# Four weight buffers of a matmul stream, moved to other addresses modulo 512 bytes

## The chip, the cores and the metric

The kernel runs on one core of one Trainium2 chip. The metric is the device time of one execution in microseconds, as the median of several runs. Beside the runs stands one execution that the hardware profiler recorded: its span is the time from its first to its last instruction, and every duration below comes from it.

## The reference

The kernel computes one layer of a trunk for a generative model: a gated linear recurrence over 2048 latent tokens and 256 context tokens of width 1024 (8 heads of 128, both directions), and behind it a gated feed-forward layer with a convolution over three positions. Cut to what matters here, the first part projects all tokens with five weight matrices a head and scans the result in chunks:

```python
def prep(h):
    q, zf_fwd, zf_bwd, v, g = jnp.split(h @ w_in, 5, axis=-1)
    q = heads(jax.nn.silu(q)); v = heads(v)
    for d, zf in enumerate((zf_fwd, zf_bwd)):
        f = lb[d] + (1.0 - lb[d]) * jax.nn.sigmoid(zf)
        logf.append(heads(jnp.log(f))); k.append(heads(1.0 - f))
    return q, k, v, logf, g

lat = lat + g1 * (rmsnorm(o, g_gain) * silu(g)) @ w_out
lat = lat + g2 * (silu(gate) * val) @ w_down      # gate, val: conv of h @ w_up
return rmsnorm(lat, final_g)
```

All of it is float32.

## The kernel before

**Matmuls in three products.** A float32 matrix is split into a high part and the rest (`split`, L77 to L81: ScalarE rounds it to float32r, VectorE subtracts), and a product is made of three float32r matmuls that add into one PSUM tile: high by high, high by rest, rest by high. In the scan these are L470, L471 and L472 of `step`: the weights `w[:, 0, k]`, `w[:, 0, k]` and `w[:, 1, k]` are the stationary operand (128 x 128), the tokens' high part, rest and high part stream past them (512 columns for a unit of four latent token tiles, 256 for the context).

**The stages.** About the first 1230 us of the span are the scan (`mixer_scan`): for two halves of the latent tokens and eight heads, five projections to a head (`project`: eight steps of k, so 24 matmuls of 512 columns), and between their steps small products: transposes (`turned`, `values`), scores inside a chunk (L673), states (L703) and outputs (L725, L728). What comes when is written out: `tick` runs an agenda after each step of three matmuls. Then comes the mixer's output (`mixer_out`, matmuls L1246 to L1248, again with transposes and small products between), to about 1489 us; then the up-projection of the feed-forward layer (`acc_mm`, L1113 to L1116, with the convolution on the other engines), to about 2305 us; then the down-projection (`product`, L1743 to L1745).

**Where the operands lie.** Tiles come from pools that stack up in SBUF. The scan's weights have the pool `wp` with four buffers of 8192 bytes a partition, `[128, 2, KT, 128]`: high and rest, eight k, 128 columns, so that every stationary operand is a run of 512 bytes and starts at the same residue modulo 512 as its buffer. The tokens lie in four blocks of 16384 bytes, `TOK = [128, UT, 2, 4, 128]` (four token tiles, high and rest, four k, 128 columns), in the pool `hp`; a moving operand is four runs of 512 bytes, 4096 bytes apart. By the addresses of the built program both the buffers of `w` and the blocks of `tok` (and the context's `cxt`) start at 96 modulo 512. In the mixer's output the stationary operand `ghl` starts at 352 and the moving `wo` at 96 (for the first of 16 token tiles the stationary tiles are `gh` and `gl`, at 96); in the up-projection the weights start at 96 and the moving operands at 352; in the down-projection the stationary `mh`, `ml` at 352 and the moving `w` at 96.

**What stands around the change.** The pool `lp` lies just below `wp` and holds one tile, `stg`. It outlives the scan, and the pools of the mixer's output begin where it ends. Above `wp` lie the scan's other pools (`hq`, `fix`, `gp`, `xp`). Buffers of `wp` are made in `load_w` (L186) and `split_head0` (L244); late in the scan two of them serve once more as `wraw` (L824), raw weights of the output projection on their way to being split.

Of the kernel before, what the change touches and what calls it, by code (L numbers as in the profile page):

```python
# [11 lines left out]
F32 = mybir.dt.float32  # L12
F32R = mybir.dt.float32r
# [8 lines left out]
D = 1024  # L22
# [3 lines left out]
KT = 8  # L26
# [10 lines left out]
V_CW, V_CB = 0, 132  # L37
V_CN = 176


UT = 4
NS = 4 * UT
# [3 lines left out]
def body(ctx, tc, a, out):  # L46
# [31 lines left out]
    def split(h, l, src):  # L78
        i = act.activation(h, src, AF.Copy)  # L79
        j = dve.tensor_tensor(l, src, h.bitcast(F32), OP.subtract)  # L80
        return i.ins, j.ins  # L81
# [13 lines left out]
    def pool_(stack, name, bufs=1, **kw):  # L95
        return stack.enter_context(tc.tile_pool(name=name, bufs=bufs, reuse_waits="tile", **kw))
# [56 lines left out]


    lp = pool_(ch, "lp")
    c1 = ctx.enter_context(ExitStack())
    wp = pool_(c1, "wp", 4)
    hq = pool_(c1, "hq")
# [23 lines left out]
    def x_tile(xt, t):  # L182
        src, r = (a["x"], t) if t >= 0 else (a["ctx"], t + 2)
        sp.dma_start(xt, src[r * 128:(r + 1) * 128])

    def load_w(h, ty):  # L186
        raw = rawp.tile([128, D], F32, name="raw", tag="raw")
        sp.dma_start(raw, a["w_in"][h, ty])
        w = wp.tile([128, 2, KT, 128], F32R, name="w", tag="w")
        split(w[:, 0], w[:, 1], raw.rearrange("p (k n) -> p k n", k=KT))  # L190
        return w

# [29 lines left out]
    with ExitStack() as c0:  # L222
# [19 lines left out]
        head0 = {}  # L242

        def split_head0(ty, raw):  # L244
            head0[ty] = w = wp.tile([128, 2, KT, 128], F32R, name="w", tag="w")
            return split(w[:, 0], w[:, 1], raw.rearrange("p (k n) -> p k n", k=KT))

        pool.memset(silp, 0.0)
# [21 lines left out]
        for k in range(KT):  # L270
            for c in range(4):
                n = 2 * k + c // 2
# [3 lines left out]
        with tc.issue_after(squared[-1]):  # L276
            made = split_head0(2, head_raw[2])
# [21 lines left out]
        def split_ctx(g):  # L299
            b = cxt[:, g // 2, :, :, 2 * (g % 2):2 * (g % 2) + 2]  # L300
            return split(b[:, :, 0], b[:, :, 1], hmc[g].rearrange("p k s n -> p s k n"))

        made = evict_ctx(0)
        order = [(evict_ctx, 1), (split_ctx, 0), (evict_ctx, 2), (split_ctx, 1), (split_head0, 1),
                 (evict_ctx, 3), (split_ctx, 2), (split_ctx, 3)]
        for f, g in order:
# [6 lines left out]
        with behind_of(made):  # L313
            for t in range(4):
                norm_begin(staged[t], late_junk, gp)
                if t == 1:
                    split_head0(3, head_raw[3])
            norm_end()
# [88 lines left out]
    def mixer_scan():  # L407
# [499 lines left out]
        def head(g, h):  # L907
            w = head0 if g == h == 0 else {}

            def weight(ty):  # L910
                if ty not in w:
                    w[ty] = load_w(h, ty)
                return w[ty]
# [190 lines left out]
    def cols(u, odd):  # L1104

        return u[:, 1:1 + HALF].rearrange("p (j o n) -> p j o n", o=2, n=128)[:, :, odd]
# [332 lines left out]
    wp = pool_(ctx, "wp")  # L1439
# [152 lines left out]
    for g, (half, s, n, q, pairs) in enumerate(todo):  # L1592
# [8 lines left out]
        w, r = pairs[q].w.pop(LEFT[n]), rhs[n]  # L1601
# [9 lines left out]
        elif n == "T1":  # L1611
# [3 lines left out]
            i = dve.tensor_tensor(cols(uvs[q], 1), u2s[q], z, OP.add).ins  # L1615
# [315 lines left out]
```

## Time and profile before

| What | Value |
|---|---|
| median of 3 runs | 2730.86 us (2729.72 to 2731.76) |
| profiled execution, span | 2729.5 us |
| TensorE clock granted in it | 0.997 |
| HBM read, written | 293.23 MB, 114.57 MB |
| DMA packets | 229104, 410.56 MB, mean 150 GB/s |

The stages in the profiled execution, by a view that cuts the span into stretches (busy us of each engine, in brackets how many instructions; then clock, share of the DMA engines, GB/s):

```profile
50.00:610.00 560.00, 558.35 (x4360) 481.58 (x4359) 351.35 (x548) 222.28 (x390) 88.17 (x236) 1.00 0.27 85
610.00:1229.00 619.00, 618.90 (x4730) 517.29 (x4729) 414.50 (x580) 193.03 (x334) 101.76 (x222) 1.00 0.41 130
1229.00:1489.00 260.00, 257.50 (x1376) 218.54 (x1375) 225.90 (x462) 156.83 (x358) 42.32 (x36) 1.00 0.87 310
1489.00:2305.00 816.00, 815.84 (x3599) 674.98 (x3598) 645.54 (x732) 378.49 (x519) 314.10 (x338) 1.00 0.33 108
2305.00:2729.50 424.50, 416.47 (x1833) 343.32 (x1831) 322.78 (x443) 166.34 (x254) 9.23 (x16) 1.00 0.70 232
```

The first number behind each stretch is its length, then come TensorE's matmuls, its weight loads, VectorE, ScalarE and GpSimd. How the profile is to be read: PE is TensorE's matmul row, PEld its weight loads, DVE VectorE, ACT ScalarE, POOL GpSimd, SP the engine that issues most DMAs. A row of the groups reads: line, engine, operation, output from inputs, shape, count, then busy us and mean ns of one, then idle time before and what ended it. The end of a matmul is modelled, so its recorded duration is longer than the time until the next one starts; the starts are as recorded.

### The profile page before, as it was taken

To read this page: it belongs to the slowest core of one execution; us is meant where nothing else is said; L and a number is where in the kernel's file an instruction comes from. 1 tells how busy PE (TensorE), PEld (TensorE's weight loads), DVE (VectorE), ACT (ScalarE), POOL (GpSimd) and SP (SyncE) were. 2 spreads that over 40 slices of the span, in tenths; PEclk is the share of its full clock that TensorE was granted. 3 is DMA by queue.
4 is the path that set the end of the run, shared out by engine and by line. 5 is a ranking of instruction groups with operands and counts; after the bars stand their busy time and mean duration, and the time that the engine had idled before them with its cause. 6 is when DMAs were issued, how large, how long until landed. Compare 5 with 4: busy or idle time off the path is not lost.

```text
span 2729.5 us, 41987 instructions
## 1 busy us (share of the span) xinstructions
PE 2698.7 (99%) x16060; PEld 2252.7 (83%) x16060; DVE 1977.8 (72%) x2803; ACT 1136.9 (42%) x1887; POOL 572.9 (21%) x885
## 2 busy tenths in 40 slices
PE   7999999999999999999999999999999999999999
PEld 4888888888888888888888888888888888888887
DVE  4756655556767776668997888777877777578896
ACT  5334444323233233335666444444444444333444
POOL 3211111011111111211211543333434440000001
PEclk8999999999999999999999999999999999999999
DMA  6213323224544443228888232228322234988653
GB/s 240 86 53 105 106 83 97 86 87 163 167 124 137 149 137 113 87 80 297 300 300 344 93 93 82 73 79 307 93 76 79 78 93 137 309 279 289 200 185 131
DMA packets 229104, 410.56 MB, mean 150 GB/s; under 512 B 29604, under 2 KB 137508, under 8 KB 225064
## 3 DMA queue, kind: packets, MB, share of 16 engines
q1 hardware_dynamic: 224152, 398.65, 44.1%
q10 hardware_dynamic: 4752, 9.24, 0.9%
q8 instruction: 126, 2.06, 0.3%
q14 instruction: 74, 0.61, 0.1%
HBM read 293.23 MB, written 114.57 MB: 149 GB/s over the span
## 4 chain that ended last, share of the span: by engine, by line
PE 91%; DMA 3%; DVE 3%; ACT 1%; issue 1%; POOL 1%; SPq 0%; ACTq 0%; POOLq 0%; DVEq 0%
PE z L470 11%; PE z L472 11%; PE z L471 11%; PE y L1744 4%; PE y L1743 4%; PE y L1745 4%; PE zc L1113 3%; PE zc L1116 3%; PE zc L1115 3%; PE zd L1113 3%; PE zd L1115 3%; PE zd L1116 3%; PE za L1116 3%; PE za L1115 3%; PE za L1113 3%; PE kv L703 2%
## 5 line engine op out<-in xcount | busy, mean ns | idle before, releaser
L470 PE MATMUL z<-tok,w 128*128 128x512 f32 x1280 | 516.4, 404 | 0.0
L472 PE MATMUL z<-tok,w 128*128 128x512 f32 x1280 | 501.0, 391 | 0.0
L471 PE MATMUL z<-tok,w 128*128 128x512 f32 x1280 | 500.6, 391 | 0.0
L80 DVE TENSOR_TENSOR w<-raw,w 128x512 fp32r<-128x512 f32 (+1 forms) x258 | 237.2, 922 | 131.7 <-ACT w L79 127.8
L472 PEld LDWEIGHTS z<-tok,w 128*128 128x128 f32 x1280 | 240.4, 188 | 52.1
L470 PEld LDWEIGHTS z<-tok,w 128*128 128x128 f32 x1280 | 240.8, 188 | 45.7 <-issue 1.7
L471 PEld LDWEIGHTS z<-tok,w 128*128 128x128 f32 x1280 | 241.1, 188 | 43.9 <-DVE tok L80 0.2
L79 ACT ACTIVATE w<-raw 128x512 fp32r<-128x512 f32 (+1 forms) x258 | 194.8, 760 | 132.9 <-PE zd L1116 75.9
L1743 PE MATMUL y<-w,mh 128*128 128x512 f32 x600 | 233.4, 390 | 1.2 <-ACT X L1777 1.2
L1744 PE MATMUL y<-w,mh 128*128 128x512 f32 x600 | 233.6, 389 | 0.2 <-DVE w L80 0.2
L1745 PE MATMUL y<-w,ml 128*128 128x512 f32 x600 | 233.4, 389 | 0.0
L546 DVE TENSOR_TENSOR_SCAN S<-F,d 128x528 f32<-128x528 f32 (+1 forms) x80 | 91.3, 1144 | 119.1 <-ACT F L525 118.9
L80 DVE TENSOR_TENSOR w<-s,w 128x512 fp32r<-128x512 f32 x126 | 121.5, 967 | 57.2 <-ACT w L79 56.3
L75 POOL TENSOR_TENSOR rs<-rs,mhalf 128x1 f32<-128x1 f32 (+3 forms) x53 | 61.9, 1168 | 417.7 <-DVE rs L74 417.7
L79 ACT ACTIVATE w<-s 128x512 fp32r<-128x512 f32 x126 | 78.5, 628 | 150.5 <-POOL s L1181 83.5
L1113 PE MATMUL zc<-rT,w 128*128 128x512 f32 x352 | 137.1, 390 | 0.2 <-DMA rT<-rhs1T 0.2
L1116 PE MATMUL zc<-rT,w 128*128 128x512 f32 x352 | 136.9, 389 | 0.0
L1115 PE MATMUL zc<-rT,w 128*128 128x512 f32 x352 | 136.9, 389 | 0.0
L1743 PEld LDWEIGHTS y<-w,mh 128*128 128x128 f32 x600 | 112.6, 188 | 25.8 <-ACT X L1777 2.1
L1744 PEld LDWEIGHTS y<-w,mh 128*128 128x128 f32 x600 | 112.6, 188 | 23.9 <-DVE w L80 0.6
L1745 PEld LDWEIGHTS y<-w,ml 128*128 128x128 f32 x600 | 112.6, 188 | 23.3
L1116 PE MATMUL za<-rB,w 128*128 128x512 f32 x336 | 130.7, 389 | 0.0
(359 smaller groups left out, 6259.0 us busy)
## 6 DMA issues: line engine op xcount, KB each, us to landing
raw<-in_w_up_dram SPq DMA_DIRECT2D x88, 512.0 KB, 4.0
raw<-in_w_in_dram SPq DMA_DIRECT2D x80, 512.0 KB, 4.0
lr<-m SPq DMA_DIRECT2D x49, 512.0 KB, 5.2
m<-r SPq DMA_DIRECT2D x66, 256.0 KB, 4.3
spare<-in_w_ada_dram SPq DMA_DIRECT2D x32, 512.0 KB, 4.2
kq<-stash SPq DMA_DIRECT2D x15, 1024.0 KB, 8.0
og<-stash SPq DMA_DIRECT2D x30, 512.0 KB, 5.3
u<-in_w_down_dram SPq DMA_DIRECT2D x51, 256.0 KB, 3.5
```

What stands on the lines that cost most here:

```text
L79: i = act.activation(h, src, AF.Copy)
L80: j = dve.tensor_tensor(l, src, h.bitcast(F32), OP.subtract)
L470: pe.matmul(z, w[:, 0, k], h, start=k == 0, stop=False, skip_group_check=True)
L471: pe.matmul(z, w[:, 0, k], l, start=False, stop=False, skip_group_check=True)
L472: stepped_pe[:] = [pe.matmul(z, w[:, 1, k], h, start=False, stop=k == KT - 1, skip_group_check=True).ins]
L546: dve.tensor_tensor_scan(flat(S[:, d]), flat(F[:, d]), flat(d1[:, 0:ns]), 0.0, OP.mult, OP.max)
L1113: pe.matmul(o, w[:, 0, k], r[:, :, 0, k], start=start and k == 0, stop=False, skip_group_check=True)
L1115: pe.matmul(o, w[:, 0, k], r[:, :, 1, k], start=False, stop=False, skip_group_check=True)
L1116: i = pe.matmul(o, w[:, 1, k], r[:, :, 0, k], start=False, stop=k == 3, skip_group_check=True)
L1743: pe.matmul(z, lh, rh, start=start, stop=False, skip_group_check=True)
L1744: pe.matmul(z, lh, rl, start=False, stop=False, skip_group_check=True)
L1745: pe.matmul(z, ll, rh, start=False, stop=stop, skip_group_check=True)
```

## The change

Three things. The pool `lp` gets one more tile, `gap`, of 64 float32 (256 bytes) a partition, ahead of `stg`; nothing reads or writes it. The buffers of `w` become 16 float32 (64 bytes) longer, and `w_tile` hands out the first 2048 elements of one in the old shape. With that the four buffers begin 256 bytes higher, and each 64 bytes further modulo 512 than the one before: at 352, 416, 480 and 32, while `tok` and `cxt` stay at 96. All scan tiles above the weights begin 512 bytes higher; the tiles of the mixer's output above `lp` begin 256 bytes higher.

```diff
+W_SHIFT, W_STEP = 64, 16
+
 UT = 4
...
     lp = pool_(ch, "lp")
+    lp.tile([128, W_SHIFT], F32, name="gap", tag="gap", bufs=1)
     c1 = ctx.enter_context(ExitStack())
     wp = pool_(c1, "wp", 4)
...
+    def w_tile():
+
+        w = wp.tile([128, 2 * D + W_STEP], F32R, name="w", tag="w")
+        return w[:, 0:2 * D].rearrange("p (i k n) -> p i k n", i=2, k=KT)
+
     def load_w(h, ty):
         raw = rawp.tile([128, D], F32, name="raw", tag="raw")
         sp.dma_start(raw, a["w_in"][h, ty])
-        w = wp.tile([128, 2, KT, 128], F32R, name="w", tag="w")
+        w = w_tile()
         split(w[:, 0], w[:, 1], raw.rearrange("p (k n) -> p k n", k=KT))
         return w
...
         def split_head0(ty, raw):
-            head0[ty] = w = wp.tile([128, 2, KT, 128], F32R, name="w", tag="w")
+            head0[ty] = w = w_tile()
             return split(w[:, 0], w[:, 1], raw.rearrange("p (k n) -> p k n", k=KT))
```

The built program has the same instructions in the same order on every engine; lines below the edit move by two to eight, and the waits are the same but for one DMA, the load of `conv` (L1374), which lies over other tiles of the scan than before.

## The prediction

> **What bounds the kernel now.** I read the page's engine shares first, then the chain of waits, then the groups of TensorE instructions kept apart by shape, and last the timeline of single matmuls. The first three lines of the page and of the clock view say which engine counts:
>
> ```profile
> PE 2698.7 (99%) x16060; PEld 2252.7 (83%) x16060; DVE 1977.8 (72%) x2803; ACT 1136.9 (42%) x1887; POOL 572.9 (21%) x885
> PE 91%; DMA 3%; DVE 3%; ACT 1%; issue 1%; POOL 1%; SPq 0%; ACTq 0%; POOLq 0%; DVEq 0%
> core 0: 2729.5 us, clock 0.997
> ```
>
> TensorE is busy 99% of the span, it makes 91% of the chain that ended last, and its clock is granted in full. So an edit that removes no matmul and no wait can only act through the pace of the matmuls, and a nanosecond on each of the scan's 3840 is worth 3.8 us. The groups, with mean ns of one behind the comma:
>
> ```profile
> L470 PE MATMUL z<-tok,w 128*128 128x512 f32 x1280 | 516.4, 404 | 0.0
> L472 PE MATMUL z<-tok,w 128*128 128x512 f32 x1280 | 501.0, 391 | 0.0
> L471 PE MATMUL z<-tok,w 128*128 128x512 f32 x1280 | 500.6, 391 | 0.0
> L1743 PE MATMUL y<-w,mh 128*128 128x512 f32 x600 | 233.4, 390 | 1.2 <-ACT X L1777 1.2
> L1113 PE MATMUL zc<-rT,w 128*128 128x512 f32 x352 | 137.1, 390 | 0.2 <-DMA rT<-rhs1T 0.2
> L1246 PE MATMUL y<-wo,ghl 128*128 128x512 f32 x240 | 96.0, 400 | 1.9 <-ACT ghl L79 1.6 <-DVE lat L1255 0.3
> L1248 PE MATMUL y<-wo,ghl 128*128 128x512 f32 x240 | 94.1, 392 | 0.0
> L1247 PE MATMUL y<-wo,ghl 128*128 128x512 f32 x240 | 93.6, 390 | 0.0
> L1246 PE MATMUL y<-wo,gh 128*128 128x512 f32 x16 | 6.4, 402 | 0.0
> ```
>
> All of these stream 512 columns past 128x128 weights. I call offset the weights' start less the moving operand's start, modulo 512, both from the addresses that the built program assigns. Before the change it is 0 in the scan (both begin at 96), and 256 in the up-projection L1113 (weights 96, moving 352), in the down-projection L1743 (352 and 96) and in the mixer's output L1246 to L1248 with ghl (352 and 96). The tempting reading is that the scan's 404/391/391 against 390 elsewhere is a collision at offset 0. But the mixer's output stands at offset 256 and shows 400/390/392, the scan's pattern, and its 16 matmuls with gh at offset 0 show 402 where ghl has 400. What the scan and the mixer's output share is not the offset but the 128-column transposes and products put between their matmuls, which the other two stages lack. The medians say that nothing is slow throughout (min/median/max ns):
>
> ```profile
> L470 PE MATMUL z<-tok,w x1280: 387/389/504, 49.4 to 1229.2; 128*128 128x512 f32 x183
> L1246 PE MATMUL y<-wo,ghl x240: 387/389/498, 1246.2 to 1461.3; 128*128 128x512 f32 x120
> ```
>
> A matmul's end is modelled, its start is not, so I take the pace from starts. The first and the last of 37 matmuls in an undisturbed stretch of the scan, of 37 in the up-projection, and of 5 with 256 columns:
>
> ```profile
> 1195.10 0.39 PE L471 MATMUL z<-tok,w 128*128 128x512 f32 x1
> 1203.26 0.39 PE L471 MATMUL z<-tok,w 128*128 128x512 f32 x1
> ```
>
> ```profile
> 1700.23 0.39 PE L1113 MATMUL zb<-rT,w 128*128 128x512 f32 x1
> 1708.39 0.39 PE L1113 MATMUL zc<-rT,w 128*128 128x512 f32 x1
> ```
>
> ```profile
> 601.06 0.28 PE L471 MATMUL z<-cxt,w 128*128 128x256 f32 x1
> 601.54 0.28 PE L472 MATMUL z<-cxt,w 128*128 128x256 f32 x1
> ```
>
> Scan at offset 0: 8.16 us over 36 steps, 226.7 ns. Up-projection at offset 256: the same 8.16 us over 36 steps. The settled pace does not differ by 0.3 ns. With 256 columns a step is 0.48 / 4 = 120 ns, so 256 columns more cost 106.7 ns and a fixed part of 226.7 - 2 x 106.7 = 13.3 ns sits in every matmul at both offsets.
>
> The unsettled steps come after small products. Two such stretches, of the scan (offset 0) and of the mixer's output (offset 256), each from its third large matmul on:
>
> ```profile
> 1184.75 0.40 PE L472 MATMUL z<-tok,w 128*128 128x512 f32 x1
> 1184.98 0.40 PE L470 MATMUL z<-tok,w 128*128 128x512 f32 x1
> 1185.22 0.39 PE L471 MATMUL z<-tok,w 128*128 128x512 f32 x1
> ...
> 1186.83 0.39 PE L472 MATMUL z<-tok,w 128*128 128x512 f32 x1
> ```
>
> ```profile
> 1325.16 0.40 PE L1248 MATMUL y<-wo,ghl 128*128 128x512 f32 x1
> 1325.40 0.40 PE L1246 MATMUL y<-wo,ghl 128*128 128x512 f32 x1
> 1325.63 0.39 PE L1247 MATMUL y<-wo,ghl 128*128 128x512 f32 x1
> ...
> 1327.24 0.39 PE L1248 MATMUL y<-wo,ghl 128*128 128x512 f32 x1
> ```
>
> Nine steps take 2.08 us in both, 231.1 ns each, and then both fall into 226.7. So the settling costs 4.4 ns a step for some ten steps, and it runs alike at offsets 0 and 256, with a moving operand in four pieces (tok) and in one (wo).
>
> **The change part by part.** It adds no instruction and removes none. Engine by engine the built programs list the same instructions in the same order; only line and buffer numbers differ.
>
> - The four weight buffers now begin at 352, 416, 480 and 32 modulo 512 against the tokens' 96: offsets 256, 320, 384 and 448. By the program 1008 of the 3840 scan matmuls read the first buffer and 2832 the other three. For the first buffer the trace has the answer: offset 256 is what the up-projection, the down-projection and the mixer's output have, so its matmuls stay at 226.7 ns settled and 231.1 while settling. Gain 0.
> - Offsets 320, 384 and 448 do not occur before with 512-column matmuls, so their cost is bounded from both sides. Gain at most: the whole fixed part, 13.3 ns x 2832 = 37.7 us. Loss at most: the larger steps of the settling kept up for good; both stretches hold a step of 0.24 us, and at that every time it is 13.3 ns x 2832 = 37.7 us the other way. I take 0, by the row that is nearest: going from offset 0 to 256 moved neither the settled pace nor the settling, and the 128-column products stand at other offsets without a mark of it:
>
> ```profile
> L703 PE MATMUL kv<-v,kt 128*128 128x128 f32 x512 | 67.9, 275 | 0.5 <-ACT sk L709 0.4
> L728 PE MATMUL o<-v,at 128*128 128x128 f32 x256 | 49.5, 275 | 0.0
> L362 PE MATMUL oi<-Sb,kq 128*128 128x128 f32 x240 | 29.3, 275 | 0.0
> ```
>
> Their offsets are 384 (kt 128, v 256), 448 (at 192, v 256) and 256 (kq 352, Sb 96), and all three take 275 ns. They are float32 with 128 columns, where the scan's are float32r with 512, so they make the price likely, not certain.
> - The split on ScalarE and VectorE writes w as often and in the same runs of 4 KB, on engines that are 42% and 72% busy and hold 1% and 3% of the chain. Price 0.
> - Behind the weights all scan tiles move by 512 bytes, so modulo 512 they stand as before. The stage after the scan starts its pool 256 bytes later; of its operands only xn (transposed) and gl of the first token tile change their residue, 128 and 16 matmuls. At 4.4 ns each that is at most 0.6 us.
> - One wait differs: the conv load L1374 now overlaps other scan tiles and waits for VectorE and TensorE where it waited for transfers.
>
> ```profile
> SPq L1374 <- DMA stash<-so: 9.9, 1, 9.9
> PE y L1246 <- ACT ghl L79: 1.6, 1, 1.6
> ```
>
> On SP's queue it stands ahead of the stash loads of the mixer's output, which themselves wait for the last stash stores; nothing reads conv until the FFN. If the queue comes free sooner, the most to win is TensorE's one idle moment there, 1.6 us; if later, the same is lost again. I take 0.
>
> Sum: 2729.5 us span + 0. The runs' median is 2730.86, 1.4 us above this execution's span, and that is what lies around it: 2729.5 + 1.4 = **2730.9 us**. A change of under 0.2% (5.5 us) is what a measurement of this kernel can't tell from none.
>
> **The rivals.**
>
> *The collision is real and goes.* Then the scan's excess over 389 ns vanishes. For L471 and L472 it is 2 ns x 2560 = 5.1 us; with L470's 15 ns x 1280 = 19.2 us it is 24.3 us. Time 2706 to 2726. For it: the scan is the one stage at offset 0 with a high mean. Against it: the mixer's output at offset 256 has the same excess, and L470's part is mostly the first matmul behind small products, whose record starts early while it waits its turn. Chance 0.15.
>
> *The fixed part is the collision.* If weight reads and moving reads meet at offsets 0 and 256 alike and miss each other at the three new ones, 13.3 ns x 2832 = 37.7 us go, and with the 456 context matmuls on those buffers 6.1 us more: 2687 to 2693. For it: 13.3 ns are there in every large matmul and no row tells their cause, and every offset in those rows is a multiple of 256. Against it: nothing in the trace varies with the offset. Chance 0.12. The Trainium skill ("TensorE: Matmul & The Clock Gate", section "Back-to-back issue gap") gives N / 2.4 + 2.5 ns for a warm isolated gap, 215.8 at 512 columns; the trace has 226.7, 10.9 more, and by that page as an estimate 2832 x 10.9 = 30.9 us would be free to win (2700). Against this rival and the next stands the skill's "SBUF — State Buffer", section "A bandwidth-pool intuition that's wrong (but worth ruling out)": weights have a second read port independent of the moving operand's. By that rule the time stays at 2730.9; the equal 226.7 ns at two offsets agree with it.
>
> *The new offsets keep the stream unsettled (slower).* The settled pace is a state that the stream falls into after some ten steps. If at 320, 384 or 448 it does not fall into step, the 2832 matmuls run at the settling's mean: 4.4 ns x 2832 = 12.5 us, 2743; at its 0.24 us steps 37.7 us, 2769. It decides from 1.9 ns a matmul (5.5 us). For it: the pace visibly depends on how the stream starts. Against it: it settled at both offsets seen. Chance 0.20.
>
> That the change doesn't do what it says I exclude: the built program has the four addresses.
>
> **How the numbers follow.** No change 0.53, first rival 0.15, second 0.12, third 0.20. Faster is 0.15 + 0.12 = 0.27, the same 0.53, slower 0.20. The likeliest case by itself spans 2726 to 2736. The range goes down to 2706, the foot of the first rival, which leaves out the second (0.12), and up to 2748, which takes in the third from its mean pace and leaves out its worse part (0.08): 0.20 left out.
>
> **What would show it.** In the groups of the changed kernel the three scan lines should read 404/391/391 again, the median 389, and undisturbed stretches 226.7 ns a step on every buffer; after small products nine steps of some 2.08 us. The first rival would show L470 to L472 nearer 389 with L1246 to L1248 unmoved; the second a median under 389 and an up-projection that keeps its own; the third a median over 389. I would be wrong if steps differ between the first buffer and the other three: then the residue by 64 bytes matters, and offsets that are multiples of 256 could not show it.

## The result, and the profile after

The changed kernel is slower by a quarter of a per cent: 2736.57 us (median of 7 runs, 2735.51 to 2739.82) against 2729.72 (7 runs, 2726.86 to 2732.01), a ratio of 1.0026 with a 95% interval of 1.0017 to 1.0036. The profiled execution took 2737.12 us, 2735.1 of them in the span.

The page's engine shares, chain of waits and clock view of the changed kernel (its lines stand eight further down: L470 to L472 are now L478 to L480):

```profile
PE 2704.9 (99%) x16060; PEld 2250.2 (82%) x16060; DVE 1976.2 (72%) x2803; ACT 1137.5 (42%) x1887; POOL 574.5 (21%) x885
PE 92%; DMA 4%; DVE 3%; ACT 1%; issue 1%; POOL 0%; SPq 0%; ACTq 0%; POOLq 0%; DVEq 0%
core 0: 2735.1 us, clock 0.999
```

TensorE is as busy as before, at the full clock, and its share of the chain went from 91% to 92%. Its busy time grew by 6.2 us with the same 16060 matmuls, so the matmuls themselves are slower. The groups by shape say which:

```profile
L478 PE MATMUL z<-tok,w 128*128 128x512 f32 x1280 | 518.9, 406 | 0.0
L480 PE MATMUL z<-tok,w 128*128 128x512 f32 x1280 | 503.9, 394 | 0.0
L479 PE MATMUL z<-tok,w 128*128 128x512 f32 x1280 | 503.9, 394 | 0.0
L1751 PE MATMUL y<-w,mh 128*128 128x512 f32 x600 | 233.4, 390 | 0.7 <-ACT X L1785 0.6
L1121 PE MATMUL zc<-rT,w 128*128 128x512 f32 x352 | 137.0, 389 | 0.2 <-DMA rT<-rhs1T 0.2
L1254 PE MATMUL y<-wo,ghl 128*128 128x512 f32 x240 | 96.0, 400 | 1.4 <-ACT ghl L81 1.4
L478 PE MATMUL z<-cxt,w 128*128 128x256 f32 x192 | 55.9, 291 | 1.3 <-ACT cxt L81 1.3
```

The scan's lines went from 404/391/391 to 406/394/394. The down-projection, the up-projection and the mixer's output, whose operands did not move against each other (but for the `gl` of one token tile), read what they read before within 1 ns. The context's matmuls (256 columns, the last row) became *shorter*; their row before was

```profile
L470 PE MATMUL z<-cxt,w 128*128 128x256 f32 x192 | 57.4, 299 | 1.3 <-ACT cxt L79 1.3
```

Most of the 8 ns in this row is not the change. The first context matmuls run between 34 and 50 us, and from 38 to 42 us the recorded execution of the kernel before had half the clock. Two rows of the view by stretches, before and then changed (the clock is the third number from the end):

```profile
38.00:42.00 4.00, 3.44 (x16) 3.44 (x17) 3.59 (x8) 3.97 (x7) 0.55 (x1) 0.50 0.57 205
```

```profile
38.00:42.00 4.00, 2.93 (x22) 2.73 (x23) 3.58 (x7) 3.71 (x7) 0.54 (x1) 1.00 0.60 209
```

The clock there is a matter of the execution, not of the offsets: in the kernel with both operands moved together (below), whose scan has the offsets of before, it is 1.00 as well. From 50 us on the row's mean falls from 293 to 290 ns only.

The view of one source line, for the scan's first matmul in the changed kernel (min/median/max ns, first and last start):

```profile
L478 PE MATMUL z<-tok,w x1280: 387/394/505, 48.3 to 1236.2; 128*128 128x512 f32 x183
```

The median rose from 389 to 394, so this is no matter of a few late matmuls. The last of them starts at 1236.2 us instead of 1229.2. These 7.0 us are more than the whole 5.6 by which the span grew; behind the scan the span is 1.4 us shorter.

Recorded durations carry a modelled end, so the pace is again read from starts. The timeline of TensorE in the changed kernel, in an undisturbed stretch (a run of large matmuls without small products between them) that passes from buffer to buffer. The first three lines read the buffer at offset 256, the next two the one at 448, the last two the one at 320:

```profile
147.48 0.40 PE L478 MATMUL z<-tok,w 128*128 128x512 f32 x1
...
149.55 0.39 PE L478 MATMUL z<-tok,w 128*128 128x512 f32 x1
...
152.73 0.39 PE L480 MATMUL z<-tok,w 128*128 128x512 f32 x1
152.95 0.39 PE L478 MATMUL z<-tok,w 128*128 128x512 f32 x1
...
158.22 0.39 PE L480 MATMUL z<-tok,w 128*128 128x512 f32 x1
158.44 0.40 PE L478 MATMUL z<-tok,w 128*128 128x512 f32 x1
...
163.81 0.39 PE L480 MATMUL z<-tok,w 128*128 128x512 f32 x1
```

and a stretch of the fourth buffer, at offset 384:

```profile
171.83 0.40 PE L478 MATMUL z<-tok,w 128*128 128x512 f32 x1
...
177.19 0.39 PE L480 MATMUL z<-tok,w 128*128 128x512 f32 x1
```

At 256 the nine steps from 147.48 take 2.07 us (230 ns each: the settling, here behind matmuls on another buffer), the fourteen from 149.55 take 3.18 us (227). Then, without a pause in the stream, 23 steps at 448 take 5.27 us (229), 23 at 320 take 5.37 us (233), and elsewhere 23 at 384 take 5.36 us (233). The pace changes where the buffer changes.

Over all 3428 steps from one such matmul to the next (leaving out the first behind a small product), sorted by buffer, the changed kernel has these mean steps:

| offset | mean step, ns | more than ten matmuls into a stretch |
|---|---|---|
| 256 | 229.0 | 227.7 |
| 320 | 233.2 | 233.3 |
| 384 | 232.5 | 232.5 |
| 448 | 229.6 | 229.2 |

(The second column at 256 still holds settling, since a buffer often begins in the middle of a stretch.)

Summed over the 3428, what lies above 226.7 ns was 5.6 us before, all of it settling, and is 14.9 us now: 9.3 us more. Of the context's 518 steps with 256 columns, the 452 behind 50 us were 120 ns and are 115.5 at 320, 118.4 at 384 and 117.8 at 448: 0.9 us less. So the offsets cost 8.4 us. The 66 context steps ahead of 50 us took 1.9 us less than before, by the clock shown above, which brings the sum to 6.5 us, against 7.0 in the scan's end. The medians differ by 6.85 us; why the span became 1.4 us shorter behind the scan no run shows.

### The profile page after: what moved, and what is told of

Its sections match the earlier page's. It is cut to its first block, busy times and chain, and to the rows that moved or that the text cites. A ratio compares the mean times of both kernels' runs of the same rounds, so it can differ in the third digit from the quotient of the medians.

```text
span 2735.1 us, 41986 instructions
## 1 busy us (share of the span) xinstructions
PE 2704.9 (99%) x16060; PEld 2250.2 (82%) x16060; DVE 1976.2 (72%) x2803; ACT 1137.5 (42%) x1887; POOL 574.5 (21%) x885
## 4 chain that ended last, share of the span: by engine, by line
PE 92%; DMA 4%; DVE 3%; ACT 1%; issue 1%; POOL 0%; SPq 0%; ACTq 0%; POOLq 0%; DVEq 0%
PE z L478 11%; PE z L480 11%; PE z L479 11%; PE y L1752 4%; PE y L1751 4%; PE y L1753 4%; PE zc L1121 3%; PE zc L1123 3%; PE zc L1124 3%; PE zd L1123 3%; PE zd L1121 3%; PE zd L1124 3%; PE za L1123 3%; PE za L1124 3%; PE za L1121 3%; PE kv L711 2%
## 5 line engine op out<-in xcount | busy, mean ns | idle before, releaser
L478 PE MATMUL z<-tok,w 128*128 128x512 f32 x1280 | 518.9, 406 | 0.0
L480 PE MATMUL z<-tok,w 128*128 128x512 f32 x1280 | 503.9, 394 | 0.0
L480 PEld LDWEIGHTS z<-tok,w 128*128 128x128 f32 x1280 | 240.4, 188 | 54.5
L478 PEld LDWEIGHTS z<-tok,w 128*128 128x128 f32 x1280 | 240.9, 188 | 48.7 <-issue 1.7
L1751 PE MATMUL y<-w,mh 128*128 128x512 f32 x600 | 233.4, 390 | 0.7 <-ACT X L1785 0.6
L1752 PE MATMUL y<-w,mh 128*128 128x512 f32 x600 | 233.5, 389 | 0.3 <-DVE w L82 0.3
L1753 PE MATMUL y<-w,ml 128*128 128x512 f32 x600 | 233.5, 389 | 0.0
```

Source lines behind the costliest of these rows:

```text
L478: pe.matmul(z, w[:, 0, k], h, start=k == 0, stop=False, skip_group_check=True)
L480: stepped_pe[:] = [pe.matmul(z, w[:, 1, k], h, start=False, stop=k == KT - 1, skip_group_check=True).ins]
L1751: pe.matmul(z, lh, rh, start=start, stop=False, skip_group_check=True)
L1752: pe.matmul(z, lh, rl, start=False, stop=False, skip_group_check=True)
L1753: pe.matmul(z, ll, rh, start=False, stop=stop, skip_group_check=True)
```

## The experiments

The theory after this result: the pace of the stream depends on the offset between the two operands' starts. The rivals: it depends on the weights' own address, or on something else that the change brought (longer buffers, other places of the tiles above). Each run is compared with the kernel before on the same chip. All edits are to the kernel before unless said otherwise.

**One offset for all four buffers.** A gap ahead of the weights, buffers of the old length, and a pad behind so that all tiles above move by 512 bytes as in the change. Once with 256 bytes:

```diff
+    before_w = pool_(c1, "before_w")
+    before_w.tile([128, 64], F32, name="gap", tag="gap", bufs=1)
     wp = pool_(c1, "wp", 4)
+    after_w = pool_(c1, "after_w")
+    after_w.tile([128, 64], F32, name="pad", tag="pad", bufs=1)
```

> All four weight buffers 256 bytes higher, of the old length: every buffer at offset 256 (weights' start less tokens' start, modulo 512), all tiles above them 512 bytes higher as in the change. Theory R (the pace hangs on the offset between weights and moving operand, modulo 256): as before the change, the three scan lines at 404/391/391 ns, settled steps 226.7 ns, time within 3 us of before. Theory P (the price is that of tiles moved along with the weights, or of the longer buffers, not of the offset): the scan lines at 406/394/394 and 5 to 8 us more, as in the change.

Once with 320 (`[128, 80]` and `[128, 48]`):

> All four weight buffers at offset 320, no buffer longer. In the trace of the change the buffer at 320 ran at 233.2 ns a step, from the first to the last. Theory R: 3428 undisturbed steps at 233.3 in place of 228.3, 17 us more in the scan's latent matmuls, 2 us less in the 256-column context matmuls (115.5 in place of 120), so about 15 us over before; the median of the three scan lines at 395 to 396 in place of 389. Theory P: no more than the change, 5 to 8 us.

Measured: at 256 2729.58 us against 2729.89, ratio 0.9999 (0.9989 to 1.0008); at 320 2743.19, ratio 1.0047 (1.0032 to 1.0062), 13.3 us more. The scan's groups, first of the kernel with all buffers at 256, then of the one with all at 320:

```profile
L474 PE MATMUL z<-tok,w 128*128 128x512 f32 x1280 | 516.4, 404 | 0.0
L476 PE MATMUL z<-tok,w 128*128 128x512 f32 x1280 | 501.0, 391 | 0.0
```

```profile
L474 PE MATMUL z<-tok,w 128*128 128x512 f32 x1280 | 521.2, 407 | 0.0
L476 PE MATMUL z<-tok,w 128*128 128x512 f32 x1280 | 505.9, 395 | 0.0
```

The timeline of the latter, from the third large matmul behind small products on:

```profile
1204.28 0.40 PE L476 MATMUL z<-tok,w 128*128 128x512 f32 x1
...
1206.38 0.40 PE L476 MATMUL z<-tok,w 128*128 128x512 f32 x1
...
1211.98 0.40 PE L476 MATMUL z<-tok,w 128*128 128x512 f32 x1
```

Nine steps take 2.10 us (233), the next 24 take 5.60 us (233): at 320 the stream has one pace from the start and never falls into 226.7. Summed as above, the steps cost 17.2 us more than before (22.8 above 226.7 against 5.6), and the 452 context steps, mostly 113 ns here, give 2.8 us back: 14.4, where 13.3 were measured. Both times are what the theory of the offset (R) gives; P does not fit the pair.

**The change in its two parts.** The longer buffers alone, so that the offsets are 0, 64, 128 and 192:

```diff
+    after_w = pool_(c1, "after_w")
+    after_w.tile([128, 64], F32, name="pad", tag="pad", bufs=1)
...
+    def w_tile():
+        w = wp.tile([128, 2 * D + 16], F32R, name="w", tag="w")
+        return w[:, 0:2 * D].rearrange("p (i k n) -> p i k n", i=2, k=KT)
...
-        w = wp.tile([128, 2, KT, 128], F32R, name="w", tag="w")
+        w = w_tile()
```

> The second half of the change alone: buffers 64 bytes longer, no gap before them, so offsets 0, 64, 128 and 192. Theory R (offset modulo 256 alone): the change's offsets 256, 320, 384, 448 are the same modulo 256, so the whole price is here: 1008 matmuls at 226.7 settled, the others at 233.3, 232.6 and 229.8; 5 to 8 us over before, scan lines 406/394/394. Theory S (it takes the shift too): within 3 us of before.

And the shift alone, as an edit to the changed kernel:

```diff
-W_SHIFT, W_STEP = 64, 16
+W_SHIFT, W_STEP = 64, 0
```

> The first half of the change alone: the gap of 256 bytes ahead of the weights where the change has it, buffers of the old length, offset 256 against the tokens and 0 against the context. Theory R: as before, scan lines 404/391/391, within 2 us. Theory S: some us over before.

Measured: the step alone 2736.99 us against 2729.62, ratio 1.0026 (1.0015 to 1.0037), the whole price; the shift alone 2729.29, ratio 1.0000 (0.9991 to 1.0009). One row of each, of the step alone and then of the shift alone:

```profile
L477 PE MATMUL z<-tok,w 128*128 128x512 f32 x1280 | 504.2, 394 | 0.0
```

```profile
L479 PE MATMUL z<-tok,w 128*128 128x512 f32 x1280 | 500.7, 391 | 0.0
```

The late steps of the step alone are 227.6 at 0, 233.2 at 64, 232.5 at 128 and 229.4 at 192. Beside the table above, 64 reads like 320, 128 like 384 and 192 like 448. So among multiples of 64 the mean pace goes by the offset modulo 256.

**Both operands moved together.** 64 bytes at the foot of the pool `hp` move weights, tokens and context alike. In the mixer's output they move `wo` but not `ghl`, which takes that stage to offset 192:

```diff
     hp = pool_(ch, "hp")
+    hp.tile([128, 16], F32, name="gap", tag="gap", bufs=1)
```

> A gap of 64 bytes at the foot of the scan's pools: weights, tokens and context all start at 160 modulo 512, offset 0 again; the mixer's output keeps ghl at 352 and has wo at 160, offset 192. Theory R (the offset between the two operands): the scan as before, 404/391/391 and 226.7 settled; the mixer's output no longer settles and runs at the 229.2 ns that the change's buffer at 448 has late in a stretch (448 is 192 modulo 256), some 1.5 us in all; time within 4 us of before. Theory A (the address of the weights by itself): the scan at 233 ns a step like the change's buffer at 416, 15 us more, the mixer's output as before.

Measured: 2729.86 us against 2729.89, ratio 0.9998 (0.9989 to 1.0008). The scan's line and the mixer's output in the groups of this kernel:

```profile
L473 PE MATMUL z<-tok,w 128*128 128x512 f32 x1280 | 500.8, 391 | 0.0
L1247 PE MATMUL y<-wo,ghl 128*128 128x512 f32 x240 | 96.9, 404 | 1.2 <-ACT ghl L79 1.2
```

The scan stays as it was with both operands 64 bytes further on: the weights' own address is not what counts. The mixer's output lost its settled pace, as its timeline shows:

```profile
1325.22 0.39 PE L1247 MATMUL y<-wo,ghl 128*128 128x512 f32 x1
...
1329.34 0.39 PE L1247 MATMUL y<-wo,ghl 128*128 128x512 f32 x1
```

18 steps in 4.12 us, 229 ns each and no better later on. Summed over the steps there this comes to 1.0 us more than before, too little to be seen in the time.

**Another stage.** The same 64 bytes at the foot of the pool that holds the up-projection's weights (nine of its eleven buffers come to stand at 320) and, in the down-projection, the moving operand (offset 192):

```diff
     wp = pool_(ctx, "wp")
+    wp.tile([128, 16], F32, name="gap", tag="gap", bufs=1)
     fa, fr, fp = [ctx.enter_context(ExitStack()) for _ in range(3)]
```

> A gap of 64 bytes at the foot of the pool that holds 9 of the 11 weight buffers of the FFN: 2940 matmuls of the up-projection go from offset 256 to 320, some 1510 of the down-projection (whose moving operand lies in these buffers, as one run of 512 columns) to 192. Scan untouched. If the offset sets the pace in every stage: up-projection 233.3 ns, 6.6 ns x 2940 = 19.4 us; down-projection 229.8 ns, 3.1 ns x 1510 = 4.7 us; about 24 us over before. If it does so only where small products break the stream: nothing, within 3 us of before.

Measured: 2753.68 us against 2728.91, ratio 1.0090 (1.0075 to 1.0106), 24.8 us. The groups of this kernel, the scan's among them, which did not move:

```profile
L471 PE MATMUL z<-tok,w 128*128 128x512 f32 x1280 | 500.6, 391 | 0.0
L1113 PE MATMUL zc<-rT,w 128*128 128x512 f32 x352 | 139.0, 395 | 0.0
L1744 PE MATMUL y<-w,mh 128*128 128x512 f32 x600 | 235.7, 393 | 2.9 <-ACT X L1778 2.9
```

A stretch of its up-projection, from a buffer still at 256 (the first two lines) to one at 320:

```profile
1699.85 0.39 PE L1116 MATMUL za<-rB,w 128*128 128x512 f32 x1
...
1701.89 0.39 PE L1116 MATMUL za<-rB,w 128*128 128x512 f32 x1
1702.12 0.40 PE L1113 MATMUL zb<-rT,w 128*128 128x512 f32 x1
...
1708.89 0.39 PE L1116 MATMUL zd<-rT,w 128*128 128x512 f32 x1
```

Nine steps of 227 ns, then 29 steps in 6.77 us, 233 ns. The up-projection has no transposes or small products between its matmuls, and it pays the same: its steps take 20.2 us more in all, those of the down-projection 3.9 us, together 24.1 of the 24.8. So the effect belongs to the operands' offset, not to the scan.

**Finer offsets.** One profiled run with buffers stepped by 32 bytes from 128 on (`[128, 32]` as the gap, `2 * D + 8` in `w_tile`):

> Buffers at offsets 128, 160, 192 and 224. Theory R with period 256: the buffer at 128 like the change's at 384 (232.5 ns late in a stretch), that at 192 like the change's at 448 (229.2); 160 between or above them; 224 is open and tells whether the pace changes by steps of 64 bytes (then as 192) or finer. Theory R with period 512: 128 and 192 show other values.

and one in which each weight tile starts at another place inside a longer buffer, by turns:

```diff
+    OFFSETS = [0, 16, 32, 48, 64, 80, 96, 112, 128, 4, 8, 12, 24]
+    made_w = []
+    def w_tile():
+        o = OFFSETS[len(made_w) % len(OFFSETS)] // 4
+        made_w.append(o)
+        w = wp.tile([128, 2 * D + 32], F32R, name="w", tag="w")
+        return w[:, o:o + 2 * D].rearrange("p (i k n) -> p i k n", i=2, k=KT)
```

> Each weight tile of the scan begins at one of many offsets modulo 256: multiples of 16 from 0 to 240 and 4, 8, 12, 24 bytes past 0 and 128, by turns over the 80 tiles. Theory R64 (the pace changes with whole steps of 64 bytes): offsets up to 63 all settle at 226.7 ns, 64 to 127 at 233.3, 128 to 191 at 232.6, 192 to 255 at 229.8. Theory Rfine (it changes with every line of 16 or 32 bytes): offsets of 16, 32 and 48 differ from 0 by 2 ns or more. In either, an offset below 226.7 would be a faster place; the largest gain to be had is the fixed part of 13.3 ns. Time between 2735 and 2745.

Measured: 2742.52 us beside 2729.89, and 2739.24 beside 2728.91. Steps more than ten matmuls into a stretch are 232.7 at 128, 233.4 at 160, 229.8 at 192 and 233.4 at 224 in the first kernel: 128 and 192 again read like 384 and 448. In the second, in ns, for 20 of the 45 offsets that occur there (24 to 95 steps each; a passage is the part of a stretch that reads one buffer, and each offset has a few):

| offset | step | offset | step | offset | step | offset | step |
|---|---|---|---|---|---|---|---|
| 0 | 227.9 | 16 | 233.2 | 96 | 234.2 | 240 | 227.6 |
| 4 | 232.3 | 24 | 230.5 | 128 | 232.3 | 256 | 226.8 |
| 8 | 230.6 | 32 | 233.1 | 132 | 226.8 | 272 | 229.2 |
| 12 | 228.1 | 64 | 233.5 | 136 | 233.2 | 388 | 231.0 |
| 260 | 232.3 | 80 | 232.0 | 192 | 233.4 | 448 | 229.0 |

Four bytes already take the stream out of 226.7 (4 and 260 alike), and none of the 45 offsets goes below it. But 16 and 272, 132 and 388, 192 and 448 differ by 4 ns, though they are equal modulo 256. The reason stands in the passages one by one. Two passages of 24 matmuls, both at offset 272, in the timeline of this kernel (first and last matmul of each):

```profile
493.25 0.40 PE L479 MATMUL z<-tok,w 128*128 128x512 f32 x1
...
498.62 0.40 PE L481 MATMUL z<-tok,w 128*128 128x512 f32 x1
...
1051.55 0.39 PE L479 MATMUL z<-tok,w 128*128 128x512 f32 x1
...
1056.77 0.39 PE L481 MATMUL z<-tok,w 128*128 128x512 f32 x1
```

23 steps take 5.37 us in the one (233.5) and 5.22 us in the other (227.0). So at some offsets there is more than one pace. The first followed a buffer at 416, the second one at 0, so what ran ahead may decide which pace the stream falls into. The offset of the buffer ahead does not decide it by itself: in the kernel with the buffers at 128 to 224, the passages at 128 that directly follow a buffer at 160 run, by their last twelve steps, at 231.7 (seven) or at 233.3 (seven). The step-only kernel has two paces at 192: of its 22 passages of 20 steps or more, 19 run at 228.8 to 229.4 at the end and three at 233.7 or 233.8. At 320 there is one pace (39 of 39 stretches of 20 steps or more at 233.3 in the kernel with all buffers there), and at 0 in the kernel before too (38 of 39 at 226.7, one at 227.5). A theory by which the offset alone fixes the pace falls, be it by its residue modulo 64 or by its exact value.

**Where another offset helps.** The context's matmuls had become faster in the change. 192 bytes below the context's tokens alone (with a pad of 320 behind) give them the offset 64 and leave the latent tokens at 0:

```diff
+    before_c = pool_(c1, "before_c")
+    before_c.tile([128, 48], F32, name="gap", tag="gap", bufs=1)
     hq = pool_(c1, "hq")
+    after_c = pool_(c1, "after_c")
+    after_c.tile([128, 80], F32, name="pad", tag="pad", bufs=1)
```

> Weights and latent tokens of the scan stay at offset 0; the context tokens alone move by 192 bytes, so that their 256-column matmuls stand at offset 64 modulo 256. In the kernel with all buffers at 320 these took 113 to 115 ns in place of 120 (3.8 us less over 518 steps). If the gain is theirs alone: 3 to 5 us under before, a ratio of 0.998 to 0.999. If it hung on what stands around them: within 1 us.

Measured: 2727.70 us against 2728.91, ratio 0.9994 (0.9986 to 1.0003). The timeline of this kernel shows the effect:

```profile
601.28 0.28 PE L474 MATMUL z<-cxt,w 128*128 128x256 f32 x1
...
602.98 0.28 PE L474 MATMUL z<-cxt,w 128*128 128x256 f32 x1
```

15 steps in 1.70 us, 113 ns where it was 120. Summed over the 452 context steps behind 50 us this is 2.4 us, 0.1% of the whole, and the time cannot tell it from nothing: the ratio is the lowest of all edits, but a gain is not shown.

**Half the weights.** Does the load of the weights set the fixed part? The third product with 64 of its 128 weight columns; it leaves out the rest-by-high term of 64 of the 128 output rows:

```diff
-            stepped_pe[:] = [pe.matmul(z, w[:, 1, k], h, start=False, stop=k == KT - 1,
+            stepped_pe[:] = [pe.matmul(z[0:64], w[:, 1, k, 0:64], h, start=False, stop=k == KT - 1,
```

> Offset 0 as before, but the third matmul of each scan step (rest by high) takes the first 64 of the 128 weight columns and writes 64 output rows: that term is left out for the other 64. Its weight load is read while the second matmul streams. Theory C (the fixed part of 13.3 ns is weight reads that hold up the moving reads): the step from the second matmul to the third falls by about half of 13.3, to 220 ns, 8.5 us in all. Theory D (a fixed cost of each matmul, whatever weights are loaded): 226.7 stays.

and the same with all buffers at 320:

> The same cut with all four buffers at offset 320, where the fixed part was 233.3 - 213.3 = 20 ns. Theory C: the step from the second matmul to the third falls by about 10 ns, to 223, 13 us under the kernel with all buffers at 320. Theory D: 233.3 stays.

Measured, in one run each: 2733.93 us beside 2729.62, and 2744.04 (all buffers at 320 with whole weights took 2743.19). The shortened load and its matmul in the source view of the kernel at offset 0:

```profile
L472 PEld LDWEIGHTS z<-tok,w x1280: 133/134/138, 49.0 to 1233.5; 128*64 128x64 f32 x183
L472 PE MATMUL z<-tok,w x1280: 387/393/476, 49.2 to 1233.8; 128*64 128x512 f32 x183
```

and a stretch of its timeline, from one half-loaded matmul to another nine rounds later:

```profile
1195.86 0.40 PE L472 MATMUL z<-tok,w 128*64 128x512 f32 x1
...
1202.07 0.39 PE L472 MATMUL z<-tok,w 128*64 128x512 f32 x1
```

27 steps in 6.21 us, 230 ns. The load is shorter (134 ns instead of 188), yet the stream at offset 0 became *slower*: it no longer settles. The step from the second matmul to the third, which by C should have fallen to 220 and 223, is 229.0 ns at 0 and 232.9 at 320. D's number came at 320 (233.3 over all steps), not at 0 (229.9 in place of 226.7). Neither theory of the cause stands as it was put. The edit also halves the rows that this matmul writes, and the runs do not tell the two apart.

## Why the prediction was wrong where it was

It forecast no change (2730.9 us); the kernel is slower by 0.26%, 6.85 us, and the interval excludes none. The 2736.57 us lie within the range of 2706 to 2748, but just above what the likeliest case spans by itself (2726 to 2736). They are inside thanks to the third rival, which had a chance of 0.20; the mechanism on which the forecast stood, that the offset does not matter, was wrong. Step by step:

- *Only the pace of the matmuls counts.* Right. The whole price is in the pace of the scan's matmuls; what lies behind the scan became 1.4 us shorter.
- *The first buffer at offset 256, price 0.* Right: the shift alone gave 1.0000, and all four at 256 gave 0.9999. In the change itself this buffer's steps became 0.5 ns longer (229.0 against 228.5 for the same buffer before): behind a buffer at another offset the stream has to settle again.
- *Offsets 320, 384 and 448, "I take 0, by the row that is nearest".* This is the step that failed. All rows with 512 columns that the profile had stood at offsets 0 and 256, and these are the same place modulo 256. Their agreement to 0.3 ns was read as "the offset has no effect", while it could only say that 256 bytes have none. The text named this gap in its last sentence and still priced it at nothing. Measured against 226.7 ns: +6.5 at 320, +5.8 at 384, +2.9 at 448. The bound set on the gain rested on a fixed part of 13.3 ns, taken from the paces at 512 and 256 columns. No run shows such a part: the same working at 320, from 233.3 and 113.3 ns, gives -6.7 ns, since the two column counts answer to the offset in different ways.
- *The 128-column products as a second witness* (275 ns at 384, 448 and 256). They did not carry over. They are of another kind, and their equality was read from durations with a modelled end: even the steps of 233 ns show in the durations only as 395 instead of 391.
- *The third rival* (the stream stays unsettled) had the mechanism: the steps at the three offsets do not fall into 226.7. Its size was 4.4 ns x 2832 = 12.5 us. The mean of the three excesses, weighted by their steps, is 5.0 ns, but 1.6 ns of settling (5.6 us over 3428 steps) had been paid before, so 3.4 ns were new. And they are not the settling's steps kept up: 320 runs at 233.3 from the start, above the settling's 231.1, and 448 below it.
- *The context's matmuls* had no term in the sum. They gave 0.9 us back in the changed kernel, where the second rival had 6.1 us. There, with 256 columns, the second rival's idea that other offsets are faster was right; with 512 columns it was wrong in sign.
- *The first rival* (a collision at offset 0 that goes) falls: no offset tried gave 512 columns a faster pace than 0. Its tempting reading of 404/391/391 was rightly refused, since the mixer's output still shows that pattern in the changed kernel.
- *The split, the moved tiles and the wait of the conv load at 0.* Nothing in the runs speaks against it: with the shift alone, which moves the tiles by 256 bytes, and with all buffers at 256, which moves the scan's by 512, the time is unchanged. The wait itself is the same to a tenth, as the waits of SP's queue in the changed kernel show (9.9 before):

```profile
SPq L1382 <- DMA stash<-so: 9.9, 1, 9.9
```

On the rule cited there from the Trainium skill, "SBUF — State Buffer", section "A bandwidth-pool intuition that's wrong (but worth ruling out)": the page gives TensorE a second, independent read port for the weights, and the prediction took this to leave no room for a price of the offset. The measurements differ from that reading (226.7 against 233.3 ns for the same matmul), and they decide. Whether the port itself is as the page has it no run shows, and the row that had agreed, 226.7 at offsets 0 and 256, could not test it.

What stays open is the cause behind the price of the offset, and with it why one offset has one pace and another two. That the weights' loads meet the moving operand's reads in some way that depends on where both start would fit an effect of the relative offset, but no run shows such a meeting; halving one load in three shortened the mean step at neither offset and spoiled the settled pace at 0. Other column counts, all three loads halved without fewer output rows, or moving operands in one piece at these offsets in the scan were not tried.

## What to carry to other kernels

Before a range of values is priced by two rows that agree, look whether these rows can differ at all: offsets 0 and 256 behave as one point here, and a third value (one profiled run at 320) would have told it. A stream of float32r matmuls that TensorE bounds is worth a look at the starts of both operands: with equal residues modulo 256 it settled at 226.7 ns here, at most others it ran up to 3% slower, and one unused tile of 64 bytes at the foot of a pool cost 24.8 us. Read such a pace from starts, and stage by stage, since the recorded durations moved by a per cent where the steps moved by three.

## What the runs showed of the hardware that was not expected

- The step from one 512-column float32r matmul to the next depends on the offset between the starts of weights and moving operand: 226.7 ns settled at 0 and 256, mostly 228 to 234 elsewhere. Four bytes are enough (232.3 ns).
- At some offsets the stream has two paces: 227.0 or 233.5 ns at 272, 229 or 233.7 at 192. What chooses between them is open; the offset of the buffer ahead alone does not.
- With 256 columns the preference is another one: 120 ns a step at offset 0, 113 at 64.
- A matmul in three with half the weight columns can slow the stream: its load took 134 instead of 188 ns, and the step went from 226.7 to 230 ns.
